# Where the masks are added: one change in five parts to a decoder step on one core

## The chip, the cores and the metric

The kernel runs on one NeuronCore of one Trainium2 chip. The metric is device time in microseconds, from launch to end; the median of several runs is given with its lowest and highest. One further execution was recorded by the hardware profiler; its page and its trace are what the numbers below come from. TensorE is called PE in the profile's rows (PEld is its weight load), VectorE DVE, ScalarE ACT, GpSimd POOL and SyncE SP.

## The reference

One step of a two-layer decoder for 256 prompt positions and 8 single-position samples that share all weights; the samples have 256 past positions in paged caches. Model width 1024, all arithmetic in float32.

```
layer 0: h = rmsnorm(x); q,k,v,bu,bv = h @ w_in0
         A: 8 heads of 64, partial rotary, causal softmax(q k^T / 8) @ v
         B: gated mixer: bv = layer_norm(gelu(bv)); per 128-chunk bv = tril(W) @ bv + b
            out = gelu(bu) * bv            (a sample opens a chunk: only W[0,0], b[0])
         x += concat(A, B) @ w_out0
layer 1: h = rmsnorm(x); q,k,v,u = h @ w_in1
         C: 8 heads, strictly causal stick-breaking attention
            z = q k^T / 8, L = softplus(z), weight = exp(z - L - sum of L of later keys before the query)
         D: causal means of u over 2, 4, 8, 16 positions, mixed by small matrices
         x += concat(C, D) @ w_out1
each layer then: x += ConvFFN(rmsnorm(x))  (2816 wide, causal depthwise conv of width 3)
y = rmsnorm(x)
```

The caches' new rows, the normalised bv rows of the samples and the conv and pooling states are outputs too.

## The kernel before

Activations lie transposed: features on the 128 partitions, the 264 positions (256 of the prompt, 8 samples) along the free dimension. All weights form one list of 1472 blocks of 128x128 in eight phases: in0, out0, ff0, dn0, in1, out1, ff1, dn1. Each block is multiplied as three products of split float32 values: the weights' rounded part `wh` with the operand's rounded part (L331) and with its remainder (L332), and the weights' remainder `wl` with the operand's rounded part (L333). So there are 4416 weight products of 128x264. `split` prepares tiles of eight blocks up to three tiles ahead: ScalarE writes `wh` (L308), VectorE writes `wl` (L309); four buffers of each. Weights arrive on SyncE's DMA queue in chunks of 8 or 16 blocks. In PSUM four banks (`mm`) take the sums of the weight products and four (`at`) everything else.

Everything else is side work, placed by hooks: `hk.at(n, f)` issues `f` after tile n of the phase (GA, VP, AVS and the like are such places). The Tile framework's scheduler then orders each engine's instructions by a simulated timeline; instructions wrapped in `tc.keep_in_program_order` keep their order among each other. The side work that the change touches:

- `s_qk`, `s_soft`, `s_tr`, `s_av`: attention of layer 0. A tile holds a pair of heads, each on 64 partitions. For each head's bank of 128x384 (first the 128 queries of the first block by 128 keys, then the second block by 256 keys) TensorE first multiplies the identity with a bfloat16 mask `maskb0` (L658) and then adds the two score products (L660, L662). VectorE takes maxima (L668, L669), ScalarE the exponentials with their sums (L671, L672), VectorE reciprocals (L673), ScalarE scales both parts (L674, L675). TensorE transposes the three 128x128 blocks (L684), ScalarE copies them out as `pT` (L685). `s_av` multiplies with the values (L496, L497) into `pav`.
- `sample_score`, `sm_soft`, `sm_tr`, `sample_av`, `sm_out`: the same for the eight samples against their cached pages: scores L453 into `sc`, own key's weight through a mask `sm` (`ow`) and four products with `hs` (L724, `pO`), values L467 (`pv_l`), and L480 (`po_l`).
- `gm_mean`, `gm_var`, `gm_norm`, `gm_tr`, `gm_gate`: the gated mixer. gelu of bv (L759), mean and variance, normalisation, the samples' rows sent out by a DMA (`out_bvn`), `v_pair` transposes (L491, copied out at L492), gate products (L786, `pf`), their bias added by VectorE (L787); the samples' own gate on GpSimd (L789), the product with bu on GpSimd (L790), then the split into `catB_h` (ScalarE, L415) and `catB_l` (VectorE, L416), which the out0 phase consumes first.
- `z_qk`, `softplus`, `z_cum`, `z_av`: attention of layer 1. The masks come from `maskb1` (L882), the scores from L884 and L886, then the cumulative sums are added into the same bank (L900, L901).

The constants (identity, masks, `sm`, `hs` and so on) are one array `CST` of 548 KB, loaded by one DMA between the first weight chunks. A helper records its operation at its own line, so L308, L309 and L331 to L333 stand for all phases.

Of the kernel before, what the change touches and what calls it, by code (L numbers as in the profile page):

```python
# [9 lines left out]
F32 = mybir.dt.float32  # L10
# [50 lines left out]
AVS = 18.5  # L61
# [111 lines left out]
def _consts():  # L173
# [19 lines left out]
    h8 = np.arange(8)  # L193
# [8 lines left out]
    add("sm", (used & (h32[:, None] // 2 == h8[None, :])).astype(f))  # L202
    add("hs", (used & ((2 * g32 + h32 % 2)[:, None] == (np.arange(512) // 64)[None, :])).astype(f))
# [20 lines left out]
def tile_decoder_step(ctx: ExitStack, tc: tile.TileContext, a):  # L224
# [237 lines left out]
    def sample_av(msk, pz, vtiles, gr, name):  # L462
        pv = at(f"pv_{name}{gr}")
        for pg in range(NPG):
            for j in range(4):
                sq = 4 * gr + j
                pe.matmul(pv[32 * j:32 * j + 32, :], pz[:, pg, sq, :], vtiles[sq][:, pg, :],  # L467
                          start=pg == 0, stop=pg == NPG - 1)
        s.activation(msk[:, gr], pv, AF.Copy)

    def sample_av_of(st, pz, vtiles, gr, name):
        return lambda: sample_av(st["msk"], pz, vtiles, gr, name)
# [15 lines left out]
    def v_pair(vt, src, t, name):  # L488
        p = at(f"vtp_{name}{t}")
        for kb in range(2):  # L490
            pe.transpose(p[:, kb * P:(kb + 1) * P], src[:, kb * P:(kb + 1) * P], ident)  # L491
        s.activation(vt[:, :, t * P:(t + 1) * P], p[:, :2 * P].rearrange("p (b d) -> p b d", b=2), AF.Copy)  # L492
# [120 lines left out]
    maskb0 = con.tile([P, 384], BF16, name="maskb0")  # L613
    maskb1 = con.tile([P, 384], BF16, name="maskb1")
# [40 lines left out]
    def s_qk(t):  # L655
        pss, hd = [at(f"S0_{2 * t + i}") for i in range(2)], heads(t)
        for ps in pss:
            pe.matmul(ps[:, :384], identb, maskb0, start=True, stop=False, skip_group_check=True)  # L658
        for ps, (qh, kh) in zip(pss, hd):
            tc.keep_in_program_order(pe.matmul(ps[:, 0:P], qh[:, 0:P], kh[:, 0:P], start=False, stop=False, skip_group_check=True))  # L660
# [5 lines left out]
    def s_soft(h, ps):  # L666
        st = sm.tile([P, 4], F32, tag="st", name=f"st0_{h}")
# [421 lines left out]
```

## Time and profile before

| | us |
|---|---|
| median of 3 runs (lowest, highest) | 622.53 (621.71, 623.77) |
| the profiled execution: device time | 623.37 |
| its span, first to last instruction | 621.0 |
| TensorE busy in the span | 599.9 (97%) |
| VectorE, ScalarE, GpSimd busy | 412.3, 349.6, 83.0 |
| mean granted TensorE clock | 0.995 |

First weight products of the phases in the trace: in0 4.50, out0 91.21, ff0 122.68, dn0 253.80, in1 317.90, out1 383.26, ff1 416.47, dn1 547.38 us.

How to read the rows: a row of a timeline gives its start in us from the span's start, its duration in us, engine, line, operation, the tile written and those read, shapes, the count of instructions in the row, and in brackets the engine's idle time before it and what ended that. A row of groups gives busy time and the mean of one instruction in ns, then idle time before them by releaser. Matmuls are pipelined, so two starts are further apart or closer than one duration says; float32 side products run as two passes and are counted as two records.

### The profile page before, as it was taken

How to read it: one execution, taken by the hardware profiler on the slowest of the kernel's cores; microseconds unless marked ns; L12 is line 12 of the kernel's file. 1: busy time of each engine (PE TensorE's matmuls, PEld its weight loads, DVE VectorE, ACT ScalarE, POOL GpSimd, SP SyncE). 2: the span in 40 equal slices, each digit the busy share in tenths (PEclk: the TensorE clock that was granted, in tenths of full speed). 3: DMA queues.
4: the chain of work that ended last, by engine and by line, in shares of the span. 5: the costliest groups of instructions: out<-in, count | busy, mean ns of one | idle time of the engine just before them, and what ended most of it. 6: DMA issues, size and time to landing. Idle time of an engine off the chain costs nothing.

```text
span 621.0 us, 12353 instructions
## 1 busy us (share of the span) xinstructions
PE 599.9 (97%) x4924; PEld 575.6 (93%) x4924; DVE 412.3 (66%) x705; ACT 349.6 (56%) x621; POOL 83.0 (13%) x113
## 2 busy tenths in 40 slices
PE   7899999998999999999999999999899999999994
PEld 5788987998999999999998997899899999999994
DVE  5996663959876676655555686296987766764432
ACT  5449763766655555644442757276665655555431
POOL 2330132325000000001110000042500000001121
PEclk9999999999999999999999999999999999999997
DMA  7996873543655455795477559945264554554501
GB/s 253 311 403 226 330 260 52 204 160 112 210 198 189 159 196 195 228 395 198 153 229 263 214 191 132 144 164 193 87 225 176 204 176 169 199 191 160 199 1 70
DMA packets 40970, 121.40 MB, mean 195 GB/s; under 512 B 17490, under 2 KB 18642, under 8 KB 29522
## 3 DMA queue, kind: packets, MB, share of 16 engines
q1 hardware_dynamic: 40050, 119.13, 59.5%
q10 hardware_dynamic: 864, 1.49, 0.7%
q8 instruction: 38, 0.62, 0.4%
q14 instruction: 18, 0.15, 0.1%
HBM read 116.67 MB, written 3.94 MB: 194 GB/s over the span
## 4 chain that ended last, share of the span: by engine, by line
PE 86%; DVE 5%; issue 2%; DMA 2%; ACT 2%; POOL 1%; SPq 0%; DVEq 0%; ACTq 0%
PE mm L331 27%; PE mm L332 26%; PE mm L333 26%; DVE wl L309 2%; DMA XG<-in_x 1%; PE pv_l L467 1%; PE sc L453 1%; DMA raw<-in_w 1%; ACT wh L308 1%; PE pav L496 1%; PE Z L900 1%; DVE xn_l L376 1%; PE Z L884 1%; POOL wk L554 0%; PE pt L684 0%
## 5 line engine op out<-in xcount | busy, mean ns | idle before, releaser
L309 DVE TENSOR_TENSOR wl<-raw,wh 128x1024 fp32r<-128x1024 f32 x183 | 229.4, 1255 | 132.5 <-ACT wh L308 131.8
L308 ACT ACTIVATE wh<-raw 128x1024 fp32r<-128x1024 f32 x183 | 193.5, 1059 | 187.7 <-PE mm L332 175.3
L331 PE MATMUL mm<-xn_h,wh 128*128 128x264 f32 x544 | 153.9, 284 | 0.0
L332 PE MATMUL mm<-xn_l,wh 128*128 128x264 f32 x544 | 153.9, 283 | 0.0
L333 PE MATMUL mm<-xn_h,wl 128*128 128x264 f32 x544 | 153.8, 283 | 0.0
L333 PEld LDWEIGHTS mm<-xn_h,wl 128*128 128x128 f32 x544 | 102.4, 188 | 0.0
L332 PEld LDWEIGHTS mm<-xn_l,wh 128*128 128x128 f32 x544 | 102.3, 188 | 0.0
L331 PEld LDWEIGHTS mm<-xn_h,wh 128*128 128x128 f32 x544 | 102.1, 188 | 0.0
L332 PE MATMUL mm<-a_l,wh 128*128 128x264 f32 x352 | 99.9, 284 | 0.0
L331 PE MATMUL mm<-a_h,wh 128*128 128x264 f32 x352 | 99.6, 284 | 0.0
L333 PE MATMUL mm<-a_h,wl 128*128 128x264 f32 x352 | 99.6, 283 | 0.0
L332 PEld LDWEIGHTS mm<-a_l,wh 128*128 128x128 f32 x352 | 66.2, 188 | 0.0
L333 PEld LDWEIGHTS mm<-a_h,wl 128*128 128x128 f32 x352 | 66.2, 188 | 0.0
L331 PEld LDWEIGHTS mm<-a_h,wh 128*128 128x128 f32 x352 | 66.1, 188 | 0.0
L331 PE MATMUL mm<-xg_h,wh 128*128 128x264 f32 x160 | 46.6, 298 | 4.5 <-ACT wh L308 2.0
L331 PE MATMUL mm<-xg_f_h,wh 128*128 128x264 f32 x160 | 46.3, 289 | 4.5 <-DVE wk L555 4.3
L332 PE MATMUL mm<-xg_l,wh 128*128 128x264 f32 x160 | 46.0, 292 | 0.0
L333 PE MATMUL mm<-xg_h,wl 128*128 128x264 f32 x160 | 44.7, 291 | 1.1 <-DVE wl L309 1.1
L332 PE MATMUL mm<-xg_f_l,wh 128*128 128x264 f32 x160 | 45.4, 284 | 0.0
L333 PE MATMUL mm<-xg_f_h,wl 128*128 128x264 f32 x160 | 45.3, 283 | 0.0
L331 PE MATMUL mm<-xg_n_h,wh 128*128 128x264 f32 x128 | 37.4, 292 | 0.0
L333 PE MATMUL mm<-xg_n_h,wl 128*128 128x264 f32 x128 | 36.8, 288 | 0.0
(266 smaller groups left out, 1071.0 us busy)
## 6 DMA issues: line engine op xcount, KB each, us to landing
raw<-in_w SPq DMA_DIRECT2D x89, 1024.0 KB, 4.8
K<-in_kt SPq DMA_DIRECT2D x32, 256.0 KB, 6.4
V<-in_vp SPq DMA_DIRECT2D x32, 256.0 KB, 5.4
raw<-in_w SPq DMA_DIRECT2D x5, 512.0 KB, 5.3
CST<-in_cst SPq DMA_DIRECT2D x1, 548.0 KB, 4.7
XG<-in_x ACTq DMA_DIRECT2D x1, 528.0 KB, 9.5
out_k<-k SPq DMA_DIRECT2D x1, 528.0 KB, 9.4
out_v<-v SPq DMA_DIRECT2D x1, 528.0 KB, 3.1
```

The costliest lines, as they stand in the source:

```text
L308: s.activation(h, src, AF.Copy)
L309: v.tensor_tensor(l, src, h.bitcast(F32), ALU.subtract)
L331: pe.matmul(o, h[:, c:c + P], xh, start=first, stop=False)
L332: pe.matmul(o, h[:, c:c + P], xl, start=False, stop=False)
L333: pe.matmul(o, l[:, c:c + P], xh, start=False, stop=left[m] == 0)
L376: j = v.scalar_tensor_tensor(l, src, gain, h.bitcast(F32), ALU.mult, ALU.subtract)
L453: pe.matmul(ps[32 * t:32 * t + 32, :PAST].rearrange("p (g k) -> p g k", g=NPG), qz[:, t, sq, :], kt[sq][:, :, t * P:(t + 1) * P], start=sq ...
L467: pe.matmul(pv[32 * j:32 * j + 32, :], pz[:, pg, sq, :], vtiles[sq][:, pg, :], start=pg == 0, stop=pg == NPG - 1)
L496: pe.matmul(o, vt[:, 0, h * HD:(h + 1) * HD], w[:, :SEQ], start=True, stop=False)
L884: tc.keep_in_program_order(pe.matmul(ps[:, 0:SEQ], kh[:, 0:P], qh[:, 0:SEQ], start=False, stop=False, skip_group_check=True))
L900: pe.matmul(ps[:, 0:384], negU, x, start=False, stop=False, skip_group_check=True)
```

## The change

1. In `s_qk` the mask products are gone. Instead VectorE adds the float32 mask `m0` to the two diagonal 128x128 blocks of the bank before the maxima, in one instruction per head.
2. The two scalings of the probabilities run on GpSimd (`g.tensor_scalar`) instead of ScalarE.
3. In `z_qk` the mask is the last product instead of the first, and covers only the two diagonal blocks: 256 columns instead of 384. `maskb0` is gone, `maskb1` is 256 wide, without the fill by GpSimd.
4. The masks `sm` (8 columns to 32) and `hs` (512 columns to 128) are arranged so that one product of 32 columns gives what four products of 8 columns gave (`pO`).
5. `v_pair` transposes one or two tiles into one bank, with one copy out of it; the callers and their places change with that. `s_av` 0 and 1 come at one place.
6. The samples' rows of bv are copied to a tile of their own on GpSimd before they are sent out, and `gm_own` does the samples' own gate with two wide GpSimd instructions ahead of the four `gm_gate`.
7. `sample_av` of layer 0 moves from 18.5 to 18.9 and its products keep their order with other pinned ones; in layer 1 both groups come at the same place and the second is pinned. Further products keep program order (`gm_gate`, `v_pair`, the first products of head pairs).

```diff
-AVS = 18.5
+AVS = 18.9
...
-    add("sm", (used & (h32[:, None] // 2 == h8[None, :])).astype(f))
-    add("hs", (used & ((2 * g32 + h32 % 2)[:, None] == (np.arange(512) // 64)[None, :])).astype(f))
+    ts = np.arange(4 * NS)[None, :]
+    add("sm", (used & (g32[:, None] == ts // NS) & (h32[:, None] // 2 == ts % NS)).astype(f))
+    add("hs", (used & (h32[:, None] % 2 == r[None, :] // HD)).astype(f))
...
-    def sample_av(msk, pz, vtiles, gr, name):
+    def sample_av(msk, pz, vtiles, gr, name, pin):
...
-                pe.matmul(pv[32 * j:32 * j + 32, :], pz[:, pg, sq, :], vtiles[sq][:, pg, :],
-                          start=pg == 0, stop=pg == NPG - 1)
+                mm = pe.matmul(pv[32 * j:32 * j + 32, :], pz[:, pg, sq, :], vtiles[sq][:, pg, :],
+                               start=pg == 0, stop=pg == NPG - 1)
+                if pin or pg or j:
+                    tc.keep_in_program_order(mm)
...
-    def v_pair(vt, src, t, name):
+    def v_pair(vt, srcs, t, name):
+        n = len(srcs)
         p = at(f"vtp_{name}{t}")
+        first = True
         for kb in range(2):
-            pe.transpose(p[:, kb * P:(kb + 1) * P], src[:, kb * P:(kb + 1) * P], ident)
-        s.activation(vt[:, :, t * P:(t + 1) * P], p[:, :2 * P].rearrange("p (b d) -> p b d", b=2), AF.Copy)
+            for i, src in enumerate(srcs):
+                mm = pe.transpose(p[:, (n * kb + i) * P:(n * kb + i + 1) * P], src[:, kb * P:(kb + 1) * P], ident)
+                if not first:
+                    tc.keep_in_program_order(mm)
+                first = False
+        s.activation(vt[:, :, t * P:(t + n) * P], p[:, :2 * n * P].rearrange("p (b d) -> p b d", b=2), AF.Copy)
...
     def masks():
-        tc.keep_in_program_order(v.tensor_copy(maskb0[:, 0:P], cst("m0")))
-        v.tensor_copy(maskb0[:, SEQ:384], cst("m0"))
-        v.tensor_copy(maskb1[:, 0:P], cst("m1"))
-        v.tensor_copy(maskb1[:, SEQ:384], cst("m1"))
-        for mk in (maskb0, maskb1):
-            g.memset(mk[:, P:SEQ], 0.0)
+        for c in range(2):
+            tc.keep_in_program_order(v.tensor_copy(maskb1[:, c * P:(c + 1) * P], cst("m1")))
...
     def s_qk(t):
         pss, hd = [at(f"S0_{2 * t + i}") for i in range(2)], heads(t)
-        for ps in pss:
-            pe.matmul(ps[:, :384], identb, maskb0, start=True, stop=False, skip_group_check=True)
-        for ps, (qh, kh) in zip(pss, hd):
-            tc.keep_in_program_order(pe.matmul(ps[:, 0:P], qh[:, 0:P], kh[:, 0:P], start=False, stop=False, skip_group_check=True))
+        for i, (ps, (qh, kh)) in enumerate(zip(pss, hd)):
+            mm = pe.matmul(ps[:, 0:P], qh[:, 0:P], kh[:, 0:P], start=True, stop=True, skip_group_check=True)
+            if i:
+                tc.keep_in_program_order(mm)
...
     def s_soft(h, ps):
+        diag = ps.rearrange("p (b k) -> p b k", k=P)[:, 0:3:2, :]
+        v.tensor_tensor(diag, diag, cst("m0").unsqueeze(1).to_broadcast([P, 2, P]), ALU.add)
...
-        s.activation(pr[:, 0:P], pr[:, 0:P], AF.Copy, scale=st[:, 2:3])
-        s.activation(pr[:, P:384], pr[:, P:384], AF.Copy, scale=st[:, 3:4])
+        g.tensor_scalar(pr[:, 0:P], pr[:, 0:P], st[:, 2:3], None, ALU.mult)
+        g.tensor_scalar(pr[:, P:384], pr[:, P:384], st[:, 3:4], None, ALU.mult)
...
-        ow = sm.tile([P, NS], F32, tag="ow", name="ow", bufs=1)
+        ow = sm.tile([P, 4 * NS], F32, tag="ow", name="ow", bufs=1)
...
-        for t in range(4):
-            pe.matmul(pO[:, t * NS:(t + 1) * NS], cst("hs")[:, t * P:(t + 1) * P], st0["ow"], start=True, stop=True)
+        pe.matmul(pO[:, :4 * NS], cst("hs"), st0["ow"], start=True, stop=True)
...
-        nc.sync.dma_start(a["bvn"], bv4[:, :, SEQ:T])
+        bvn = sm.tile([P, 4, NS], F32, tag="bvn", name="bvn", bufs=1)
+        g.tensor_copy(bvn, bv4[:, :, SEQ:T])
+        nc.sync.dma_start(a["bvn"], bvn)
...
-        v_pair(st0["vgt"], bv4[:, t, :], t, "sgu")
+        v_pair(st0["vgt"], [bv4[:, t, :], bv4[:, t + 1, :]], t, "sgu")
+
+    def gm_own():
+        wide = lambda n: vec(n).unsqueeze(2).to_broadcast([P, 4, NS])
+        bs = bv4[:, :, SEQ:T]
+        g.tensor_tensor(bs, bs, wide("w00"), ALU.mult)
+        g.tensor_tensor(bs, bs, wide("b00"), ALU.add)
...
-        g.tensor_scalar(bv4[:, t, SEQ:T], bv4[:, t, SEQ:T], vec("w00")[:, t:t + 1], vec("b00")[:, t:t + 1], ALU.mult, ALU.add)
...
+    for t in (0, 2):
+        hk.at(GT, gm_tr, t)
+    hk.at(GA, gm_own)
     for t in range(4):
-        hk.at(GT, gm_tr, t)
         hk.at(GA, gm_gate, t)
-    for t in range(3):
-        hk.at(VP + t, lambda t=t: v_pair(vt, v4[:, t, :], t, "v0"))
-        hk.at(SAV + t, s_av, t) if t < 2 else None
-    hk.at(AVS, sample_av_of(st0, PZ, vtiles, 0, "l0"))
-    hk.at(AVS, sample_av_of(st0, PZ, vtiles, 1, "l0"))
+    hk.at(VP + 1, lambda: v_pair(vt, [v4[:, 0, :], v4[:, 1, :]], 0, "v0"))
+    hk.at(VP + 2, lambda: v_pair(vt, [v4[:, 2, :]], 2, "v0"))
+    for t in range(2):
+        hk.at(SAV + 1, s_av, t)
+    for gr in range(2):
+        hk.at(AVS, sample_av_of(st0, PZ, vtiles, gr, "l0", True))
...
     def z_qk(t):
...
-        for ps in pss:
-            pe.matmul(ps[:, :384], identb, maskb1, start=True, stop=False, skip_group_check=True)
-        for ps, (qh, kh) in zip(pss, hd):
-            tc.keep_in_program_order(pe.matmul(ps[:, 0:SEQ], kh[:, 0:P], qh[:, 0:SEQ], start=False, stop=False, skip_group_check=True))
+        for i, (ps, (qh, kh)) in enumerate(zip(pss, hd)):
+            mm = pe.matmul(ps[:, 0:SEQ], kh[:, 0:P], qh[:, 0:SEQ], start=True, stop=False, skip_group_check=True)
+            if i:
+                tc.keep_in_program_order(mm)
...
+        for ps in pss:
+            tc.keep_in_program_order(pe.matmul(ps.rearrange("p (b k) -> p b k", k=P)[:, 0:3:2, :], identb,
+                                               maskb1.rearrange("p (b k) -> p b k", k=P), start=False, stop=False, skip_group_check=True))
...
-    for t in range(3):
-        hk.at(13 + t, lambda t=t: v_pair(vt, v4[:, t, :], t, "v1"))
-    hk.at(14, z_av, 0)
-    hk.at(15, z_av, 1)
-    hk.at(15, z_av, 2)
+    hk.at(14, lambda: v_pair(vt, [v4[:, 0, :], v4[:, 1, :]], 0, "v1"))
+    hk.at(15, lambda: v_pair(vt, [v4[:, 2, :]], 2, "v1"))
+    for t in range(3):
+        hk.at(15, z_av, t)
...
-    hk.at(ZSA, sample_av_of(st1, PZ, vtiles, 0, "l1"))
-    hk.at(ZSA + 1, sample_av_of(st1, PZ, vtiles, 1, "l1"))
+    for gr in range(2):
+        hk.at(ZSA, sample_av_of(st1, PZ, vtiles, gr, "l1", gr == 1))
```

The weight products, their order and the preparation of the weights are as before; the feed-forward phases are not touched.

More of the change, by code (lines that the diff above doesn't have):

```diff
@@ L192, in _consts @@
     r = np.arange(P)
-    h8 = np.arange(8)
     global _ROPE
@@ L611, in tile_decoder_step @@
     v.tensor_tensor(rope[:, 1, :], CS[:, 1, :], R, ALU.mult)
[L613 to L614 removed]
+    maskb1 = con.tile([P, SEQ], BF16, name="maskb1")
     identb = con.tile([P, P], BF16, name="identb")
     def masks():
[L618 to L623 removed]
+        for c in range(2):
+            tc.keep_in_program_order(v.tensor_copy(maskb1[:, c * P:(c + 1) * P], cst("m1")))
         v.tensor_copy(identb, ident)
@@ L785, in gm_gate @@
         for c in range(2):
-            pe.matmul(pf[:, c * P:(c + 1) * P], st0["vgt"][:, c, t * P:(t + 1) * P], sguc[:, 0, t, :], start=True, stop=True)
+            mm = pe.matmul(pf[:, c * P:(c + 1) * P], st0["vgt"][:, c, t * P:(t + 1) * P], sguc[:, 0, t, :], start=True, stop=True)
+            if t or c:
+                tc.keep_in_program_order(mm)
         v.tensor_tensor(bv4[:, t, :SEQ].rearrange("p (c t) -> p c t", c=2), pf[:, :SEQ].rearrange("p (c t) -> p c t", c=2),
                         sguc[:, 1, t, :].unsqueeze(1).to_broadcast([P, 2, P]), ALU.add)
-        g.tensor_scalar(bv4[:, t, SEQ:T], bv4[:, t, SEQ:T], vec("w00")[:, t:t + 1], vec("b00")[:, t:t + 1], ALU.mult, ALU.add)
         g.tensor_tensor(bu4[:, t, :], bu4[:, t, :], bv4[:, t, :], ALU.mult)
```

9 lines of the change are left out of this document (5 added, 4 removed).

## The prediction

> **What bounds the kernel.** I read the page first: busy shares, then the chain that ended last, then the costliest groups (line, engine, operation, tile and shape, count | busy us, mean ns | idle before it and its releaser).
>
> ```profile
> span 621.0 us, 12353 instructions
> PE 599.9 (97%) x4924; PEld 575.6 (93%) x4924; DVE 412.3 (66%) x705; ACT 349.6 (56%) x621; POOL 83.0 (13%) x113
> PE 86%; DVE 5%; issue 2%; DMA 2%; ACT 2%; POOL 1%; SPq 0%; DVEq 0%; ACTq 0%
> L309 DVE TENSOR_TENSOR wl<-raw,wh 128x1024 fp32r<-128x1024 f32 x183 | 229.4, 1255 | 132.5 <-ACT wh L308 131.8
> L308 ACT ACTIVATE wh<-raw 128x1024 fp32r<-128x1024 f32 x183 | 193.5, 1059 | 187.7 <-PE mm L332 175.3
> ```
>
> TensorE is busy for 97% of the span and makes 86% of the chain. The weight split that feeds it is ahead: ScalarE's rounding (L308) waits 175.3 us for TensorE to give a buffer back, and VectorE's remainder (L309) waits for ScalarE. So the time moves by TensorE's side products (all but the weight products L331 to L333) and by TensorE's stalls. The stalls that the change touches, with the busy time of the two stretches of in0 where it works (columns: us, then busy us of each engine with its instructions, granted clock, DMA share, GB/s):
>
> ```profile
> 38.00:56.00 18.00, 17.73 (x146) 15.91 (x146) 13.85 (x38) 14.86 (x47) 2.78 (x3) 1.00 0.89 339
> 56.00:75.00 19.00, 19.00 (x197) 17.00 (x196) 10.72 (x20) 14.87 (x29) 1.10 (x2) 1.00 0.72 262
> L331 PE MATMUL mm<-catB_h,wh 128*128 128x264 f32 x64 | 17.5, 289 | 0.7 <-ACT catB_h L415 0.7
> L658 PE MATMUL S<-maskb,identb 128*128 128x384 bf16 x8 | 2.3, 332 | 0.3 <-ACT p L672 0.3
> ```
>
> From 38 to 56 us VectorE has 4.15 us left of 18.00 and ScalarE 3.14. GpSimd is nearly idle there.
>
> **The change, part by part.** Price of a side product: from the start of the first to the start of the next weight product, plus what that one takes over its usual 0.12 us.
>
> ```profile
> 33.99 0.28 PE L331 MATMUL mm<-xg_h,wh 128*128 128x264 f32 x1
> 34.12 0.50 PE L658 MATMUL S<-maskb,identb 128*128 128x384 bf16 x2
> 34.32 0.42 PE L332 MATMUL mm<-xg_l,wh 128*128 128x264 f32 x1
> 34.58 0.28 PE L333 MATMUL mm<-xg_h,wl 128*128 128x264 f32 x1
> ...
> 42.39 0.32 PE L658 MATMUL S<-maskb,identb 128*128 128x384 bf16 x1 [0.28 <-ACT p L672]
> ...
> 44.54 0.49 PE L660 MATMUL S<-k,q 64*128 64x128 f32 x4
> 44.86 0.60 PE L662 MATMUL S<-k,q 64*128 64x256 f32 x4
> 45.39 0.39 PE L331 MATMUL mm<-xg_h,wh 128*128 128x264 f32 x1
> ```
>
> Two masks cost 0.20 (34.12 to 34.32) and 0.14 on the product behind (0.26 where 0.12 is usual): 0.34, or 0.17 each. A pair of heads takes 0.32 for both first products (44.54 to 44.86; each head uses 64 rows and the two heads run side by side), 0.53 for both second ones, and about 0.1 on leaving.
>
> *Scores of in0.* The eight masks go. By the order of the instructions heads 0 to 3 stay together: 4 × 0.17 = 0.68 saved. For heads 4/5 and 6/7 the first product of the even head is now issued alone, 13 and 16 products ahead. What one head alone costs shows where the kernel already splits a pair, in in1:
>
> ```profile
> 352.79 0.70 PE L884 MATMUL Z<-q4b,k4b 64*128 64x256 f32 x4
> 353.33 0.39 PE L886 MATMUL Z<-q4b,k4b 64*128 64x128 f32 x4
> ...
> 360.80 0.70 PE L884 MATMUL Z<-q4b,k4b 64*128 64x256 f32 x2
> 361.43 0.45 PE L900 MATMUL Z<-Lh,negU 128*128 128x384 f32 x1
> ```
>
> One head alone takes 0.63, two together 0.54: a partner is free. A lone 128-column product is half the streaming of a 256-column one (0.32 against 0.53 in the pair: 0.21 less): 0.42, with 0.1 on leaving 0.52. Before, a split pair paid a lone mask 0.17, the other mask 0.27 (44.27 to 44.54, its change of form in it), 0.85 and 0.1: 1.39. After: 0.52 + 0.85 + 0.1 = 1.47. The two pairs lose 0.08 each, so the scores gain about 0.5. The wait at 42.39 is for a bank that head 0's exponentials free (0.28, with its change of form 0.4). It goes in that place; what may come instead is priced below.
>
> *Own-key weights.* Four products of eight columns become one of 32.
>
> ```profile
> 66.98 0.95 PE L724 MATMUL pO<-ow,CST 128*128 128x8 f32 x8
> 67.79 0.37 PE L331 MATMUL mm<-xg_h,wh 128*128 128x264 f32 x1
> ```
>
> 0.81 for eight passes, 0.2 for the two that stay: -0.6. VectorE's `ow` widens to 32 columns, covered by its idle time (8.28 us of 19.00 from 56 to 75).
>
> *Transposes.* Two tiles per bank save ScalarE three copies, and on TensorE only fewer interruptions: -0.1 at the gate. The head transposes of in0 are issued in smaller groups than before, +0.15.
>
> *What replaces the masks and ScalarE's scaling.* Nearest rows:
>
> ```profile
> L787 DVE TENSOR_TENSOR bv<-pf,sguc 128x256 f32<-128x256 f32 x4 | 1.5, 417 | 0.0
> L674 ACT ACTIVATE p<-p,st 128x128 f32<-128x128 f32 x8 | 3.2, 400 | 0.0
> L675 ACT ACTIVATE p<-p,st 128x256 f32<-128x256 f32 x8 | 4.0, 506 | 0.0
> L789 POOL TENSOR_SCALAR bv<-bv,VEC 128x8 f32<-128x8 f32 x4 | 1.7, 449 | 9.3 <-DMA out_bvn<-bv 9.3
> L747 POOL TENSOR_TENSOR sguc<-sguc,tril 128x512 f32<-128x512 f32 x1 | 1.3, 1278 | 3.1 <-DMA sguc<-in_sguw 3.1
> ```
>
> VectorE gains eight additions of 128x256 out of a bank, as L787's: 8 × 0.417 = 3.3 us into 4.15 us of idle. ScalarE loses 3.2 + 4.0 = 7.2 us. GpSimd gains sixteen scalings that no row shows: not under the 8-column one (0.449), not over two-input work by L747 (2.5 ns a column: 0.32 + 0.64 on a base which I leave at 0.35 each, 1.66 a head). I take 1.3 a head, nearer the upper end since it has one input: 10.4 us into a queue with 15 us free from 38 to 56, where the `sguc` product (1.28) stands between heads 0 and 1. ScalarE's pair took about 0.7 a head in line.
>
> TensorE now waits in other places: head 4's bank needs head 0's exponentials, 0.42 later by the addition; the transposes need GpSimd. The sample scores (L453), first at 57.33, move 18 products later in the order, and their bank is freed by ScalarE's copy of head 2's transpose, which now stands behind these:
>
> ```profile
> 57.33 3.66 PE L453 MATMUL sc<-K,qz_l 128*32 128x256 f32 x64
> 59.17 1.28 ACT L759 ACT_TABLE_LOAD   x1
> 60.46 1.08 ACT L759 ACTIVATE bv<-bv 128x1056 f32<-128x1056 f32 x1
> ```
>
> TensorE alone reaches them at 57.33 + 18 × 0.12 - 0.9 saved = 58.6; the copy, with the 1.28 and 1.08 ahead of it begun some 2.5 us sooner since scalings are gone, ends near 59.5. That would be 0.9 of waiting. I take 0.5, between it and none, as the copy's place behind the gelu depends on VectorE's bv, and 0.2 at head 4: +0.7 (ends 0 and 5). In0 together: -0.5 - 0.4 - 0.6 + 0.15 + 0.7 = -0.65.
>
> *Between in0 and out0.*
>
> ```profile
> 85.61 1.73 POOL L789 TENSOR_SCALAR bv<-bv,VEC 128x8 f32<-128x8 f32 x4 [9.31 <-DMA out_bvn<-bv]
> ...
> 87.99 0.43 DVE L643 TENSOR_TENSOR v<-mm,R_n 128x264 f32<-128x264 f32 x1 [1.84 <-PE mm L333]
> ...
> 89.03 3.26 POOL L790 TENSOR_TENSOR bu<-bu,bv 128x264 f32<-128x264 f32 x3 [1.70 <-ACT vt L492]
> ...
> 87.79 1.95 PE L786 MATMUL pf<-sguc,vgt 128*128 128x128 f32 x16
> ...
> 91.21 0.76 PE L331 MATMUL mm<-catB_h,wh 128*128 128x264 f32 x4 [0.66 <-ACT catB_h L415]
> L467 PE MATMUL pv_l<-V,PZ 128*32 128x512 f32 x64 | 7.5, 597 | 0.0
> ```
>
> From the gate products at 87.79 to catB_h 3.42 us pass, and TensorE has 2.76 of work. The changed order puts transposes and both groups of sample values (L467, 16 passes, about 0.9 a group) ahead of, or just behind, the first catB products, 4.0 in all, and they wait for nothing near: the work is the same, the 0.66 goes (bounds 0 and -0.9). The own-key gate on GpSimd no longer waits for the 9.31 us DMA; nobody was late for it, nothing gained.
>
> *In1 and out1.* The mask is issued last over 256 columns instead of first over 384: 0.11 for 0.17 each, -0.4 for eight. Splits move. Heads 2/3 and 6/7 now send the even head's first product alone: 0.63 + 0.1 for a lone mask's 0.17, less the later mask's cheaper place: +0.5 each. Heads 4/5 (360.80), which had four changes of form, are whole again in one group: -0.65. Behind in1 the order puts transposes, sample values and two pairs of `pav` heads together, with some eight changes of form fewer at 0.1: -0.75. Together, with 0.2 of overlap taken off the masks, -0.6 (ends -1.2 and +0.5).
>
> *Start.* The constants shrink from 548 to 368 KB ahead of a weight chunk that feeds the rope: 0 to -0.5, I take -0.2.
>
> Sum: -0.65 - 0.1 - 0.65 - 0.6 - 0.2 = -2.2. The profiled execution took 623.37 (span 621.0 and 2.4 around it), 0.84 over the median 622.53 of the runs: 621.2 in its place, 620.3 on the median.
>
> **Rivals.** *No new waits* (in0 has the slack for all of them): -2.9, 619.6. For it: ScalarE is 7.2 us lighter. Against: VectorE is left 0.9 us of idle.
>
> *The gains hide.* Sample scores wait for the table load and gelu wherever TensorE stands, and in1's splits cost what its masks save: -2.2 + 0.4 + 1.2 = -0.6, 621.9.
>
> *Slower: GpSimd and VectorE block each other.* They did in in0:
>
> ```profile
> 38.00 0.75 POOL L640 TENSOR_TENSOR rz_k<-rz_k,rope 128x264 f32<-128x264 f32 x1 [2.73 <-DVE rz_k L635]
> ...
> 38.09 1.74 DVE L309 TENSOR_TENSOR wl<-raw,wh 128x1024 fp32r<-128x1024 f32 x1
> ```
>
> L309 took 1.74 against its mean 1.255, 0.49 more, under a GpSimd operation with 0.66 left. Four L309 fall among 10.4 us of scalings; if each is held for a head's 1.3 us, VectorE needs 13.85 + 3.3 + 5.2 = 22.4 of 18.0: 4.4 us late, and with it bv, gelu and the sample scores. On top of the 0.9 above that is 619.6 + 0.9 + 4.4 = 624.9. It decides once the holds pass 2.9 us together (0.9 that VectorE has left and 2.0 up to the 622.5 of before).
>
> The Trainium skill, "SBUF — State Buffer", section "Who interferes with whom", says that a VectorE instruction with two SBUF inputs and a GpSimd instruction that reads SBUF share a port under an exclusive lock, so that the later one blocks fully. The two rows above agree within 0.2 us (0.49 of 0.66), and by that rule the time would be the 624.9 of this rival.
>
> **How the numbers follow.** The forecast 0.42, no new waits 0.20, hidden 0.20, blocking 0.18. About 0.3%, 1.9 us, is what a measurement here can tell. The forecast lies 0.3 beyond that edge: 0.25 of it counts as faster, 0.17 as the same. No new waits is faster, hidden the same, blocking (2.4 over) slower but for 0.01: faster 0.45, same 0.38, slower 0.17. The range runs down to 617.9: no new waits (619.6) with in1 (-0.6), the boundary (-0.25) and the start (-0.3) at their lower ends, and 0.5 if a lone head costs no more than its share of a pair. It runs up to 625.4: blocking, with half of the 1.1 that lies between in1's term and its upper end.
>
> **What would show it.** Right: no mask rows in in0; the row of catB_h without its 0.7; one `pO` row of two; a new TensorE wait of 0.5 to 1 us at L453's counterpart. Wrong: scalings over 0.85 us each or L309 over 1.6 us between 42 and 58 (then slower), or transposes that wait for GpSimd for over 1 us. A front of out0 that still waits would make it 621.0.

## The result, and the profile after

The changed kernel takes 625.01 us (median of 6 runs, 624.07 to 625.77); the kernel before took 622.90 beside it (621.71 to 623.77). The ratio is 1.0034, 95% interval 1.0020 to 1.0049: slower by 2.1 us, where 620.3 was forecast. A second set of runs gave 1.0043 (1.0028 to 1.0058).

The profiled execution of the changed kernel took 624.07 us, 0.94 under its median; that of before (623.37) was 0.47 over its own. So the two traces differ by 1.3 us of span only. The page, the same lines as of before:

```profile
span 622.3 us, 12329 instructions
PE 600.6 (97%) x4910; PEld 576.1 (93%) x4910; DVE 417.0 (67%) x711; ACT 344.1 (55%) x601; POOL 98.9 (16%) x126
PE 84%; DVE 7%; issue 3%; ACT 3%; DMA 2%; POOL 1%; SPq 0%; DVEq 0%; ACTq 0%; POOLq 0%
L309 DVE TENSOR_TENSOR wl<-raw,wh 128x1024 fp32r<-128x1024 f32 x183 | 230.0, 1258 | 131.0 <-ACT wh L308 130.9
```

TensorE's busy time did not fall, although it has 14 records fewer. Its new waits, from the view of waits (engine, line, releaser: us in total, times, longest), and the two stretches of in0:

```profile
PE S L662 <- ACT p L678: 1.2, 1, 1.2
PE pt L690 <- POOL p L680: 0.9, 1, 0.9
...
PE pt L690 <- POOL p L681: 0.2, 1, 0.2
```

```profile
38.00:56.00 18.00, 15.94 (x120) 13.97 (x116) 15.95 (x40) 9.37 (x30) 11.05 (x12) 1.00 0.86 330
56.00:75.00 19.00, 18.80 (x192) 16.48 (x192) 11.97 (x24) 14.04 (x29) 8.31 (x9) 1.00 0.64 232
```

Between 38 and 56 us TensorE is busy for 1.79 us less (the first two waits lie there, 2.06 together), VectorE for 2.1 more and GpSimd for 8.3 more, and ScalarE, which lost its scalings, is half idle. The wait for catB_h (0.7 before) is gone, and so is the one at the sample scores that was feared:

```profile
L331 PE MATMUL mm<-catB_h,wh 128*128 128x264 f32 x64 | 17.8, 291 | 0.0
```

Where the 1.3 us of the traces lie is told best by the place of the weight products: the start of the n-th of the 4416 rows of L331 to L333, read off each trace. Side work changes places among them, so single stretches inside in0 mean little; sums over a stage do.

```
weight product      160    420    672   2298   2874   4300    end
before            33.40  79.35 122.68 323.24 421.80 597.24 621.0
changed           31.78  79.28 122.34 323.47 421.97 598.17 622.3
changed by stage  -1.62  +1.55  -0.27  +0.57  -0.06  +0.76  +0.38
```

The stages are: start and first products of in0; the rest of in0 up to its normalisation; the boundary and out0; ff0 and dn0; in1 and out1; ff1 and dn1; the rest. Two losses stand out. In0 gives back all that the start gained, and the feed-forward phases, which the change does not touch, lose 1.3 us without any new wait. The end (+0.38) is the landing of the last output: TensorE's last sum (612.47 before, 613.45 changed) and ScalarE's first issue of an output transfer (615.55 and 616.52) are both some 0.97 later, hardly more than product 4300 (0.93).

The start's gain is not safe. Three programs with before's start (before, before_shift, before_slot) have product 160 at 33.40, 34.63 and 32.46; the five with the changed in0 (the changed kernel twice, after_pad, after_pin, scale_act) at 31.78, 31.95, 32.33, 32.32 and 33.27. The medians, which are over many executions, are therefore the judge of the size, and the traces of the place.

### The profile page after: what moved, and what is told of

Read it like the earlier page. It is cut to its first block, busy times and chain, and to the rows that moved or that the text cites. A ratio compares the mean times of both kernels' runs of the same rounds, so it can differ in the third digit from the quotient of the medians.

```text
span 622.3 us, 12329 instructions
## 1 busy us (share of the span) xinstructions
PE 600.6 (97%) x4910; PEld 576.1 (93%) x4910; DVE 417.0 (67%) x711; ACT 344.1 (55%) x601; POOL 98.9 (16%) x126
## 4 chain that ended last, share of the span: by engine, by line
PE 84%; DVE 7%; issue 3%; ACT 3%; DMA 2%; POOL 1%; SPq 0%; DVEq 0%; ACTq 0%; POOLq 0%
PE mm L331 26%; PE mm L332 26%; PE mm L333 25%; DVE wl L309 2%; DMA raw<-in_w 2%; PE pv_l L467 1%; ACT wh L308 1%; PE pav L505 1%; PE Z L899 1%; DVE xn_l L376 1%; PE sc L453 1%; PE Z L920 1%; POOL wk L563 0%; POOL p L681 0%; DVE xg_l L376 0%
## 5 line engine op out<-in xcount | busy, mean ns | idle before, releaser
L309 DVE TENSOR_TENSOR wl<-raw,wh 128x1024 fp32r<-128x1024 f32 x183 | 230.0, 1258 | 131.0 <-ACT wh L308 130.9
L333 PE MATMUL mm<-xn_h,wl 128*128 128x264 f32 x544 | 154.2, 284 | 0.0
L331 PE MATMUL mm<-xn_h,wh 128*128 128x264 f32 x544 | 153.8, 283 | 0.0
L331 PEld LDWEIGHTS mm<-xn_h,wh 128*128 128x128 f32 x544 | 102.4, 188 | 0.0
L333 PEld LDWEIGHTS mm<-xn_h,wl 128*128 128x128 f32 x544 | 102.3, 188 | 0.0
L333 PE MATMUL mm<-a_h,wl 128*128 128x264 f32 x352 | 99.8, 284 | 0.0
L331 PE MATMUL mm<-a_h,wh 128*128 128x264 f32 x352 | 99.5, 283 | 0.0
L333 PEld LDWEIGHTS mm<-a_h,wl 128*128 128x128 f32 x352 | 66.2, 188 | 0.0
L331 PEld LDWEIGHTS mm<-a_h,wh 128*128 128x128 f32 x352 | 66.2, 188 | 0.0
L331 PE MATMUL mm<-xg_f_h,wh 128*128 128x264 f32 x160 | 46.2, 289 | 4.5 <-DVE wk L564 4.3
L331 PE MATMUL mm<-xg_h,wh 128*128 128x264 f32 x160 | 46.1, 295 | 3.5 <-ACT wh L308 1.9
L333 PE MATMUL mm<-xg_h,wl 128*128 128x264 f32 x160 | 44.5, 290 | 1.3 <-DVE wl L309 1.3
L333 PE MATMUL mm<-xg_f_h,wl 128*128 128x264 f32 x160 | 45.3, 283 | 0.0
L331 PE MATMUL mm<-xg_n_h,wh 128*128 128x264 f32 x128 | 37.2, 291 | 0.0
L332 PE MATMUL mm<-xg_n_l,wh 128*128 128x264 f32 x128 | 36.9, 288 | 0.0
```

The source lines that it names most:

```text
L309: v.tensor_tensor(l, src, h.bitcast(F32), ALU.subtract)
L331: pe.matmul(o, h[:, c:c + P], xh, start=first, stop=False)
L332: pe.matmul(o, h[:, c:c + P], xl, start=False, stop=False)
L333: pe.matmul(o, l[:, c:c + P], xh, start=False, stop=left[m] == 0)
```

## The experiments

All runs are told by their label. Each median has the kernel before timed beside it; ratios with 95% intervals.

**again**: the changed kernel, unedited.

> The changed kernel once more, unedited. Theory (waits in in0): the waits of the first trace come back within 0.2 us each: 1.16 at head 4's first score product, 0.90 and 0.20 at transposes behind GpSimd's scaling; TensorE gains at the start of in0 (up to its 160th weight product 1.6 ahead of before in the first trace) are partly the luck of the weight transfers and shrink towards 0.5. Rival (the weight products themselves are slower in the changed program): from weight product 800 to 2100 and from 3200 to 4300 the trace is again 0.5 to 0.7 later than that of before. Time 624 to 626.

Measured: 624.88, ratio 1.0043. The waits are 1.03, 0.90 and 0.20, and from weight product 672 on the two traces run alike within 0.06 us up to product 4300. So neither loss is an accident of one execution. The gain at the start, expected to shrink towards 0.5, stayed at 1.45.

**scale_act** and **mask_pe** undo one half of in0's change each, **in0_back** undoes both:

```diff
 scale_act
-        g.tensor_scalar(pr[:, 0:P], pr[:, 0:P], st[:, 2:3], None, ALU.mult)
+        s.activation(pr[:, 0:P], pr[:, 0:P], AF.Copy, scale=st[:, 2:3])
 mask_pe
+        for ps in pss:
+            pe.matmul(ps[:, :384], identb, maskb0, start=True, stop=False, skip_group_check=True)
-        v.tensor_tensor(diag, diag, cst("m0").unsqueeze(1).to_broadcast([P, 2, P]), ALU.add)
```

> The changed kernel with the two scalings of the probabilities back on ScalarE; the additions of the mask stay on VectorE. Theory (waits in in0): the waits on GpSimd (0.90 and 0.20) go, the transposes are again issued in whole groups (0.6), the wait at head 4 stays near 1.2: 625.0 - 1.5 = 623.5 (ends 622.5 to 624.5). Rival (VectorE's additions alone are the loss): no change, 625.0 within 0.5. Rival (the loss lies in the weight products of the later phases): 625.0 within 0.7.

> The changed kernel with in0's masks back as first products on TensorE (eight of 384 columns), without VectorE's additions; the scaling stays on GpSimd. Theory (waits in in0): the wait at head 4 shrinks from 1.16 to some 0.3, eight masks come back (1.4 less what the split pairs cost, about 0.5 to 1), the waits on GpSimd stay or grow by 0.5 since TensorE arrives sooner: 625.0 within 0.8. Rival (VectorE's additions alone are the loss): 623.0 or less.

> Both undone: masks on TensorE and scaling on ScalarE in in0 as before; the own-key weights in one product, the transposes of two tiles, the order between in0 and out0, in1's masks and the start stay as in the changed kernel. Theory (waits in in0): in0 is as before but for the 0.65 of the own-key weights, 0.1 of the transposes and up to 0.66 between in0 and out0: 622.9 - 1.3 = 621.6 (ends 620.6 to 622.6), so faster than before. Rival (weight products slower for another reason): 624 or more.

Measured: scale_act 630.98 (1.0132, 1.0113 to 1.0150), mask_pe 623.13 (1.0011, 1.0000 to 1.0022), in0_back 622.69 (1.0010, 0.9999 to 1.0021). The theory was wrong on scale_act by 7.5 us. Its trace shows why undoing a part is no clean subtraction here: the scheduler, with ScalarE loaded again, lets the mixer's normalisation fall so late that its transposes stand at the end of in0 and wait there.

```profile
PE vtp_sgu L497 <- DVE bv L781: 3.0, 1, 3.0
...
PE sc L453 <- issue: 1.3, 1, 1.3
PE S L662 <- ACT p L678: 1.2, 1, 1.2
```

Between weight products 476 and 530 it loses 6.4 us to the kernel before. Mask_pe is 1.8 us below the changed kernel timed with it (624.88), 1.1 below the range of its theory and 0.1 above the rival's 623.0. Its wait at head 4 was expected at 0.3 and stayed at 1.17, with no addition left on VectorE (what this wait hangs on is told behind the experiments); the waits for GpSimd fell to 0.2. In0_back was forecast at 621.6 and came 1.1 over: by its trace it is 1.1 us ahead of the changed kernel behind out0 (121.21 against 122.34 at product 672, with a later start), but then loses the same 1.3 us in the feed-forward phases.

**after_pad**, **in0_back_pad** and **before_shift** ask whether those 1.3 us come from the addresses of the pools as a whole: the change shrank two constant tiles, and every later pool moved down by 2464 bytes.

```diff
 after_pad, in0_back_pad: constants 360 columns wider, the mask tile where it was
-    CST = con.tile([P, _CST_ARR.shape[1]], F32, name="CST")
+    CST = con.tile([P, _CST_ARR.shape[1] + 360], F32, name="CST")[:, :_CST_ARR.shape[1]]
 before_shift
+    CST = con.tile([P, _CST_ARR.shape[1] + 408], F32, name="CST")[:, :_CST_ARR.shape[1]]
```

> The changed kernel with two constant tiles widened by what the change took off (360 float32 columns unused behind the constants, 512 bfloat16 columns before the mask), so that every later pool in SBUF starts at the address that it has in the kernel before; order and work unchanged. Theory (addresses): the weight products of both feed-forward layers, 0.6 and 0.7 us slower in every variant of the changed kernel, are back at the pace of before: from weight product 800 to 2100 and from 2874 to 4300 within 0.1 of before, time 625.0 - 1.3 = 623.7. Rival (the pace follows from which slot of the pool the operands got, or from something else): no change, 625.0 within 0.4.

> The kernel with in0's masks and scaling as before (run in0_back), with the same widened constant tiles. Theory (addresses): 622.7 - 1.3 = 621.4, faster than before by about 0.8. Rival (slots or else): 622.7 within 0.4.

> The kernel before with its constant tile widened by 408 unused float32 columns, so that the later pools start exactly 4096 bytes above where the changed kernel has them. Theory (addresses, by their lower bits): the feed-forward phases become 1.3 us slower, 622.3 + 1.3 = 623.6. Rival (slots or else): 622.3 within 0.4.

Measured: 624.69 (1.0033, 1.0019 to 1.0046), 622.56 (0.9998, 0.9984 to 1.0012) and 622.80 (1.0000, 0.9984 to 1.0017). No pace changed: after_pad loses 0.58 and 0.77 where the changed kernel lost 0.57 and 0.76. The pools' common address is not the cause. What pace means can be read off a stretch of windows that holds weight products only (columns as above: TensorE is busy throughout, so the count in its bracket is its pace). Before, then changed:

```profile
160.00:240.00 80.00, 80.00 (x664) 80.00 (x663) 57.52 (x102) 46.86 (x86) 0.76 (x1) 1.00 0.54 186
448.00:538.00 90.00, 90.00 (x749) 90.00 (x748) 66.81 (x118) 52.30 (x97) 1.51 (x2) 1.00 0.54 188
```

```profile
160.00:240.00 80.00, 80.00 (x660) 80.00 (x660) 57.18 (x101) 46.66 (x86) 0.75 (x1) 1.00 0.54 185
448.00:538.00 90.00, 90.00 (x744) 90.00 (x743) 66.21 (x118) 52.31 (x98) 1.51 (x2) 1.00 0.55 188
```

Four products fewer in 80 us and five in 90, at the same granted clock of 1.00 and under the same load of the other engines. In ns for a tile of 24 products: 2900 before and 2917 changed in ff0, 2893 and 2913 in ff1. The pattern inside a tile repeats to the nanosecond from tile to tile in before, and with a period of two tiles in the changed kernel.

**after_pin** asks whether the wait at head 4 comes from VectorE's order.

```diff
-        v.tensor_tensor(diag, diag, cst("m0").unsqueeze(1).to_broadcast([P, 2, P]), ALU.add)
+        k = tc.keep_in_program_order
+        k(v.tensor_tensor(diag, diag, cst("m0").unsqueeze(1).to_broadcast([P, 2, P]), ALU.add))
         (the two maxima likewise)
```

> The changed kernel with VectorE's addition and two maxima of each head kept in program order, so that no head's addition is issued ahead of an earlier head's maxima. Theory (the wait at head 4, 1.03 to 1.16, comes from two or three additions standing ahead of head 0's maxima): that wait shrinks by 0.7 to 0.9; the waits for GpSimd stay: 625.0 - 0.8 = 624.2 (ends 623.6 to 624.9). Rival (the wait is VectorE's load as a whole): the wait stays over 0.8.

Measured: 623.50 (1.0020, 1.0007 to 1.0034), 1.4 us better, but not as expected: the wait at head 4 grew to 1.38, and those for GpSimd fell to 0.26. VectorE still issued the additions of heads 0 and 2, a rotary addition and an L309 ahead of head 0's maxima (43.41). So the pins left two additions and the L309 in front of the maxima, and this run does not tell what the additions cost; what it gained stands at the waits for GpSimd (1.10 to 0.26).

**before_slot**, **in0_back_slot** and **in0_back_rows** move only the operand of the feed-forward products, the normalised activations. They lie in four slots of a pool of 24 slots of 4224 bytes (rounded and remainder part of each half), given out in the order in which slots come free, and the change altered that order.

```diff
 before_slot, in0_back_slot
         def normalise(m):
+            if m == 0:
+                g.memset(f4(f"dum{l}")[:, 0, 0:1], 0.0)
 in0_back_rows
-            operand_tile(xn[m // 4], m, z, gain[:, m:m + 1])
+            operand_tile(xn[m % 2], m // 2, z, gain[:, m:m + 1])
```

> The kernel before with one more buffer of the pool of 24 touched ahead of the first normalised operand of each feed-forward phase (one GpSimd fill of one column). It moves that phase's operands to other slots: in layer 0 to slots 18, 15, 11, 6, where the changed kernel has 18, 15, 11, 7 and before has 16, 18, 1, 11. Theory (the pace of the weight products follows from where the moving operand lies): between weight products 900 and 1728 the kernel before now loses about the 0.57 us that the changed kernel loses there; time up to 1 us over before. Rival (number or order of instructions): no change there (within 0.05).

> Run in0_back (masks and scaling of in0 as before) with the same extra buffer: slots 15, 1, 7, 6 in layer 0, 11, 18, 8, 2 in layer 1. Theory (place of the operand): the pace between 900 and 1728 and between 2874 and 3888 changes by 0.1 or more against in0_back, sign not known. Rival: no change.

> Run in0_back with the eight rows of the normalised feed-forward operand dealt to the two tiles by turns (even, odd) instead of by halves: same work, other addresses. Theory (place of the operand): the pace of the feed-forward phases changes by 0.1 or more, sign not known. Rival: no change.

Measured: 623.39 (1.0022, 1.0001 to 1.0043), 621.64 (0.9991, 0.9981 to 1.0001) and 622.68 (1.0012, 1.0002 to 1.0022). Before_slot, whose only edit is a GpSimd fill of one column in each layer, took over most of the slow pace (between products 900 and 1728 it loses 0.45 us to before, the changed kernel 0.56), and in0_back_slot got the fast one back in ff1. First before_slot, then in0_back_slot:

```profile
160.00:240.00 80.00, 80.00 (x661) 80.00 (x660) 56.80 (x100) 47.06 (x87) 0.76 (x1) 1.00 0.53 187
448.00:538.00 90.00, 90.00 (x745) 90.00 (x744) 66.39 (x118) 51.74 (x96) 1.39 (x2) 1.00 0.52 188
```

```profile
160.00:240.00 80.00, 80.00 (x660) 80.00 (x659) 57.27 (x101) 46.53 (x86) 0.75 (x1) 1.00 0.53 185
448.00:538.00 90.00, 90.00 (x749) 90.00 (x748) 66.85 (x118) 52.34 (x98) 1.52 (x2) 1.00 0.52 188
```

Dealing the rows out otherwise changed next to nothing (ff0 2916.7 for 2917.0, ff1 the same). The slots and paces:

```
                     ff0: slots, ns a tile      ff1: slots, ns a tile
before               16 18  1 11   2900.0       19 22 23  2   2893.3
changed              18 15 11  7   2917.0       22  1  5  8   2913.3
mask_pe              18 15 11  7   2917.0       22  1  4 12   2906.6
before_slot          18 15 11  6   2913.3       22  1  2  3   2907.2
in0_back_slot        15  1  7  6   2919.9       11 18  8  2   2893.3
(order: rounded and remainder of rows 0 to 3, then of rows 4 to 7)
```

So the slots set the pace; that is shown. In these ten cells the same pattern of even and odd numbers gives the same pace (even, odd, odd, even: 2913.3 in two kernels), and the two fastest cells have both remainders in even slots. Slots are 4096 + 128 bytes apart and the weight buffers 4096, as the compiled program places them, so even and odd slots differ in how they lie against the weights. Whether it is that, and why it matters inside TensorE, no run here tells.

**masks_back** is in0_back and also undoes part 3, the masks of in1 as last products.

```diff
     def z_qk(t):
+        for ps in pss:
+            pe.matmul(ps[:, :384], identb, maskb1, start=True, stop=False, skip_group_check=True)
...
-        for ps in pss:
-            tc.keep_in_program_order(pe.matmul(ps.rearrange("p (b k) -> p b k", k=P)[:, 0:3:2, :], identb,
-                                               maskb1.rearrange("p (b k) -> p b k", k=P), start=False, stop=False, skip_group_check=True))
```

> Run in0_back with in1's masks as first products of 384 columns too, as before. What stays of the change: own-key weights in one product, two tiles per bank, the order between in0 and out0, the pins. If in1's masks last over 256 columns gain what was forecast of them (0.4 of the masks less the splits), this is up to 0.4 slower between weight products 2418 and 2640 than in0_back; if the splits of pairs cost what they save, it is the same within 0.2, or faster. The feed-forward phases keep the pace of in0_back.

Measured: 621.66 (0.9991, 0.9981 to 1.0000). From product 2298 to 2874 it is 0.66 us faster than before (97.90 against 98.56 us), where the changed kernel gained 0.06. So putting in1's masks last cost 0.6 us; what it meets is the splitting of pairs.

**mask_alone**, **scale_alone** and **mask_and_scale** put one part, or both, on the kernel before, by the same edits as in the diff of scale_act and mask_pe the other way round.

> The kernel before with one part alone: in0's masks added by VectorE, no mask products there; scaling stays on ScalarE; all else as before, the operands in slots of the same parity as before, so the feed-forward phases should keep their pace. If VectorE's additions are the loss by themselves: slower by 2 to 6 us (with the scaling on ScalarE the changed kernel took 631). If it is the meeting of the additions with other parts of the change (pins, gate order) that cost 6: within 1 us of before.

> The kernel before with the scaling alone moved to GpSimd; masks stay products on TensorE. By mask_pe against in0_back (0.4 slower, a wait for GpSimd of 0.19): 0 to 0.6 slower than before. If GpSimd's scaling is what costs in in0: over 1 us slower.

> The kernel before with the additions on VectorE and the scaling on GpSimd, all else as before. If the additions are the loss and GpSimd's scaling takes part of it back: 0.5 to 2.5 us slower than before, from waits at head 4's scores and at transposes, and below mask_alone. If the rest of the change matters: same as before within 0.5.

Measured: 623.22 (1.0013, 1.0001 to 1.0026), 623.21 (1.0009, 0.9994 to 1.0023) and 623.37 (1.0010, 0.9995 to 1.0025), each 0.9 to 1.0 over the 622.34 beside them; only the first is clear of no change. In their traces the stretch from product 160 to 530, in0's end and the boundary, loses 1.58, 1.56 and 1.57 us, with the feed-forward phases at the pace of before (2900 and 2893). So the additions lose on the old kernel too, with either scaling. For the scaling alone that is not shown: 1.17 of its 1.56 us are there by product 220, before TensorE has needed a scaled part, and fast (below), whose in0 has neither part, has lost 1.16 at the same place. Mask_and_scale was expected below mask_alone and is not, within the noise. Their waits, in that order:

```profile
PE sc L453 <- issue: 1.2, 1, 1.2
PE S L655 <- ACT p L671: 0.8, 1, 0.8
...
PE pf L785 <- ACT vgt L492: 0.4, 1, 0.4
```

```profile
PE S L658 <- ACT p L672: 1.2, 1, 1.2
...
PE pt L684 <- POOL p L675: 0.2, 1, 0.2
```

```profile
PE S L655 <- ACT p L671: 0.8, 1, 0.8
PE pt L683 <- POOL p L673: 0.8, 1, 0.8
```

With the additions and ScalarE's scaling, ScalarE's chain to the sample scores is late; with GpSimd's scaling that wait goes and one for GpSimd comes. The 6 us of scale_act are thus a meeting with the rest of the change, not the price of the additions.

**fast** is masks_back with the extra buffer in layer 1 only.

```diff
         def normalise(m):
+            if m == 0 and l == 1:
+                g.memset(f4(f"dum{l}")[:, 0, 0:1], 0.0)
```

> Run masks_back (the change without its masks and its scaling) with one extra buffer touched ahead of the feed-forward operand of layer 1 only: slots 1, 0, 12, 2, so both remainders in even slots, as in the two runs whose second feed-forward phase went at 2893 ns a tile. Theory (slots): 2913 back to 2893 ns a tile there, 0.55 us; time 621.7 - 0.55 = 621.1, faster than before. Rival (the pace follows the exact slots): 2900 to 2920, time 621.3 to 621.9.

Measured: 621.22 against 622.34, ratio 0.9981 (0.9970 to 0.9992): faster than both kernels. Its ff1 runs at 2893.3 ns a tile. It keeps of the change the own-key weights in one product, two transposed tiles per bank and the order between in0 and out0, and leaves out the masks and the scaling.

## Why the prediction was wrong, point by point

**Masks and scores of in0 (-0.5), the wait at head 4 (-0.4, then +0.2).** The masks' own gain came: from product 160 to 200 the changed kernel is 0.78 faster, mask_alone 0.67, for 0.68 forecast. The step that failed is "It goes in that place; what may come instead is priced below", with 0.2 for head 4. The wait of 0.28 became 1.16. The first maxima and head 0's first exponentials before:

```profile
40.79 0.27 DVE L668 TENSOR_REDUCE st<-S 128x1 f32<-128x128 f32 x1
...
41.42 0.37 ACT L671 ACTIVATE p<-S,st 128x128 f32<-128x128 f32 x1 [2.35 <-DVE st L669]
```

And after, VectorE's rows, then ScalarE's and TensorE's:

```profile
41.67 0.42 DVE L672 TENSOR_TENSOR S<-S,CST 128x256 f32<-128x256 f32 x1
42.01 0.42 DVE L645 TENSOR_TENSOR k<-k,rz_k 128x264 f32<-128x264 f32 x1
42.35 0.75 DVE L672 TENSOR_TENSOR S<-S,CST 128x256 f32<-128x256 f32 x2
43.02 0.27 DVE L674 TENSOR_REDUCE st<-S 128x1 f32<-128x128 f32 x1
```

```profile
43.66 0.37 ACT L677 ACTIVATE p<-S,st 128x128 f32<-128x128 f32 x1 [6.87 <-DVE st L675]
...
44.62 0.48 PE L662 MATMUL S<-k,q 64*128 64x128 f32 x2 [1.16 <-ACT p L678]
```

One addition costs what was forecast (418 ns by its group, for 417). But I moved the chain by one addition, 0.42, and it moved by 2.24 (41.42 to 43.66), as three additions stood ahead of the first maxima and L309 ahead of them. TensorE's own arrival moved by 1.35 only (42.11 to 43.46): head 4's place went from behind weight product 211 to behind 241, with 0.68 of masks less on the way.

Not all of the 0.88 belongs to the additions, though. The wait is as long in three kernels that have none: 1.17 in mask_pe, 1.24 in scale_alone, 1.25 in fast. Before, then fast, both with masks and scaling as before:

```profile
25.24 1.06 ACT L308 ACTIVATE wh<-raw 128x1024 fp32r<-128x1024 f32 x1 [1.98 <-DMA raw<-in_w]
26.34 1.23 DVE L309 TENSOR_TENSOR wl<-raw,wh 128x1024 fp32r<-128x1024 f32 x1 [0.58 <-ACT wh L308]
```

```profile
25.82 1.06 ACT L308 ACTIVATE wh<-raw 128x1024 fp32r<-128x1024 f32 x1 [3.32 <-DMA raw<-in_w]
26.91 1.23 DVE L309 TENSOR_TENSOR wl<-raw,wh 128x1024 fp32r<-128x1024 f32 x1 [1.92 <-ACT wh L308]
...
42.97 0.32 PE L669 MATMUL S<-maskb,identb 128*128 128x384 bf16 x1 [1.25 <-ACT p L683]
```

This is the sixth L309 of each trace. It waits for ScalarE's rounding, and that, in these rows, for weights to land. From it to the first maxima VectorE takes 14.4 to 14.5 us in all ten traces of the left half below, and 17.4 to 18.1 in the right half. So head 4 waits longer by as much as this L309 starts late (us; before_shift, where this L309 did not wait, has no wait at head 4 either):

```
masks on TensorE   VectorE idle   wait at     additions on VectorE   VectorE idle   wait at
                   before L309    head 4                             before L309    head 4
before_slot           0.57         0.24       after_pad                 0.54         0.94
before                0.58         0.28       again                     0.62         1.03
masks_back            0.65         0.32       mask_alone                0.69         0.82
in0_back_pad          1.10         0.75       mask_and_scale            0.71         0.84
in0_back              1.14         0.83       changed                   0.77         1.16
in0_back_slot         1.25         0.94       scale_act                 0.85         1.22
in0_back_rows         1.35         1.05       after_pin                 0.95         1.38
mask_pe               1.50         1.17
scale_alone           1.74         1.24
fast                  1.92         1.25
```

On the left the wait is 0.3 to 0.35 below the idle time (more in the last two, which waited 0.1 earlier on the way); in the changed kernel and its variants it is about 0.4 above. By these traces the additions, with the order that they bring, make the wait 0.7 longer when the weights land alike, an estimate, and that is all that the masks had saved; the other 0.2 of the 0.88 go with the longer idle time (0.77 for 0.58). After_pin's wait grew in the same way: measured from the idle time, pinning hardly changed it (0.43 above, 0.39 in the changed kernel). Whether a landing belongs to the kernel or to the one execution traced is not shown. ScalarE's idle time (6.87) shows that relieving it was worth nothing at this place: it waited for VectorE.

**GpSimd's scaling (1.3 us a head, no wait).** This step failed too: the sum has no wait of TensorE for GpSimd, and there were 1.10 us of it. Sixteen scalings took 16.5 us, 2.06 a head:

```profile
45.71 1.54 POOL L680 TENSOR_SCALAR p<-p,st 128x128 f32<-128x128 f32 x1 [5.38 <-DVE st L679]
47.23 0.92 POOL L681 TENSOR_SCALAR p<-p,st 128x256 f32<-128x256 f32 x1
48.12 1.28 POOL L752 TENSOR_TENSOR sguc<-sguc,tril 128x512 f32<-128x512 f32 x1
49.38 1.57 POOL L680 TENSOR_SCALAR p<-p,st 128x128 f32<-128x128 f32 x1
...
51.84 0.60 POOL L680 TENSOR_SCALAR p<-p,st 128x128 f32<-128x128 f32 x1
```

```profile
45.55 1.23 DVE L309 TENSOR_TENSOR wl<-raw,wh 128x1024 fp32r<-128x1024 f32 x1
...
51.01 0.33 PE L690 MATMUL pt<-CST,p 128*128 128x128 f32 x1 [0.90 <-POOL p L680]
```

Undisturbed a head is 0.60 + 0.92 = 1.52, over my 1.3 and under the upper end of 1.66. The rest is blocking: the scaling that began at 45.71 stood until L309 ended (45.55 + 1.23 = 46.78) and took its 0.60 from about there to 47.25. So the mechanism of the rival was right and its loser mostly wrong: GpSimd's scalings waited for VectorE, and L309's mean hardly moved (1258 ns for 1255). One L309 did lose, to the `sguc` product that had started ahead of it at 48.12. The Trainium skill, "SBUF — State Buffer", section "Who interferes with whom", has it that issue order decides who blocks, and these rows agree: the one that started first ran at its full speed, and the other was held, the scaling at 45.71 for 0.94 and the L309 at 48.72 for 0.5. That the rival's 624.9 lies beside the measured 625.0 is chance. The signs named for being wrong came: scalings of 1.03 us on average, the L309 of 1.76 and transposes that waited 1.10.

VectorE waited for GpSimd in another way, which I had not thought of. The tile `st` has three buffers, and the fourth head's maxima need the one that head 0's scaling still reads:

```profile
48.18 0.29 DVE L674 TENSOR_REDUCE st<-S 128x1 f32<-128x128 f32 x1 [0.86 <-POOL p L681]
...
48.72 1.76 DVE L309 TENSOR_TENSOR wl<-raw,wh 128x1024 fp32r<-128x1024 f32 x1
```

What this wait cost TensorE was not tested.

**Transposes (+0.15).** That term was too small: the lone groups of head transposes cost 2.32 us where they cost 1.66, and the group at the sample scores 0.22 more, as the scaled parts arrive one by one and TensorE takes single blocks between weight products.

**Own-key weights (-0.65 with the gate's -0.1).** Right: with the products beside it the group went from 1.57 to 0.89 us, -0.68, in every variant that kept it.

**Sample scores (+0.5).** Wrong: no wait; TensorE came later (59.74 for 58.6), after the waits above.

**Between in0 and out0 (-0.66).** The wait went, the gain was 0.27. The step "the work is the same" failed: the new order enters and leaves the short products oftener, some 0.4 us.

**In1 (-0.6).** It gained 0.06. The part behind in1 was right, -0.66 in masks_back for -0.75. The masks' part was wrong: a lone first product costs 0.82 with its entry, not 0.73, and there are three, since heads 4/5, which I took for whole, are split too (products 2512 and 2517). One of them, between weight products in the trace of after:

```profile
347.43 0.70 PE L899 MATMUL Z<-q4b,k4b 64*128 64x256 f32 x2
348.05 0.39 PE L331 MATMUL mm<-xg_n_h,wh 128*128 128x264 f32 x1
```

**The feed-forward phases (nothing).** Not in the sum at all, and over half of the median's loss: 0.56 us in ff0 and 0.60 in ff1 from the slots of an operand that the change does not touch. Another 0.17 lies in dn1 (products 3888 to 4300) and is not explained.

**The start (-0.2).** Hidden in its own scatter of 1 us and more; not settled. The rest of in0 adds up: its waits grew by 1.98, and the time that side products add to 0.121 us a weight product, waits taken out, fell by 0.39 (13.63 to 13.25); that is 1.6 for the 1.55 of the trace.

## What to carry to other kernels

An operation moved off the bounding engine must be followed to the next thing that engine waits for: TensorE gave up its masks and lost what they had cost at the next bank, waiting for the longer chain on VectorE. A wait can also be as long without the edit, so before one is put down to it, see what stood ahead of the wait in every trace: here one late chunk of weights moved it by 1 us. A part that is taken out or put back under a scheduler changes the order elsewhere, so prove a part both ways, on the new kernel and alone on the old one. And when untouched phases change pace without a wait, look at where their buffers came to lie.

## What the runs showed that I had not expected

The pace of the same weight products, with the same order and the same granted clock, runs from 2893 to 2920 ns for a tile of 24, by the pool slots of their moving operand alone; one unused buffer made ff1 20 ns a tile faster in two kernels (0.65 and 0.67 us) and 14 slower in a third. A common shift of all pools by 2464 bytes moved it by nothing.
